# A two-layer transformer trunk on one NeuronCore: the second layer's feed-forward begun with five blocks ahead, its first products set among the sums of its operands, and its weight splits put on VectorE

## The chip, the core and the metric

The kernel runs on one NeuronCore of one Trainium2 chip. Five engines work side by side: TensorE (PE, matrix products), VectorE (DVE), ScalarE (ACT), GpSimd (POOL), and SyncE (SP), whose queue issues nearly all of the transfers here. Each engine takes its instructions in the order in which they stand in its program; one that waits holds up all behind it on that engine. The metric is the device time of one execution in microseconds (us). Three runs of the kernel before took 2861.15, 2862.23 and 2865.08 us; their median is 2862.23.

## The reference

The input is a sequence of 1024 tokens of 1024 features with a context of 256 tokens. Two layers, each a token mixer and a gated feed-forward, with residuals and a modulation by a condition; layer 0 mixes by latent attention and a chunked MLP, layer 1 by retention and window attention. All in float32. The change touches the end of layer 1:

```python
def _swiglu(x, w_in, w_out):
    a, b = jnp.split(x @ w_in, 2, axis=-1)
    return (jax.nn.silu(a) * b) @ w_out
# layer 1, where the context has no feed-forward any more
x = x + mx[2] * yx                                   # yx = (...) @ cd_out
x = x + mx[5] * _swiglu(_modulate(_rms(x, norm_ffn[layer]), mx[3], mx[4]), ffn_in[layer], ffn_out[layer])
return _rms(x, norm_final)
```

`w_in` is 1024 x 5632 (two halves of 2816), `w_out` 2816 x 1024.

## The kernel before

Features lie on partitions, tokens along the free dimension, in two chunks of 512 tokens (0 and 1). A float32 product is made of three matmuls: each operand is split into a high part (ScalarE, an Identity to float32r) and a low part (the difference, VectorE or GpSimd), and high x high, low x high and high x low are added up in one PSUM bank (`mm3`, L112 to L114). Every product of 128 x 128 by 128 x 512 is so three matmuls.

Layer 1's mixer ends in eight output blocks for each chunk (`MixerOut.block`, L801): 24 matmuls on a weight of 512 KB, an addition into x on VectorE (L808), a square on ScalarE (L198), and for chunk 1 five of the eight squares are added into one tile on GpSimd (L202). For each block a weight is loaded and split (`load_w`, L255): high part L103, low part L107 on VectorE or L109 on GpSimd.

The feed-forward of layer 1 uses a Strassen scheme of the Winograd kind: seven products of half size in place of eight. Its operands from x are seven combinations of the two chunks, here named B11 and B21 (from chunk 0 alone), and T2, T3, T1, T4, B22 (which need chunk 1 as well). Each has four tiles, each tile with a high and a low part: 12 matmuls for each operand and block. `Seven.second` (L1466) makes the last five one after the other: scalings (L1433), subtractions (L1471, L1477), high parts (ACT L1448) and low parts (DVE L1454, L1456).

The 2816 hidden features are 22 blocks j. The front of a block is its two products with B11 and B21 (`front_1`, `front_2`; ScalarE takes the first out in `front_s`, L1609, VectorE adds the second and ScalarE makes the gate in `front_3`, L1615 and L1616). Its later products are the five with T2, T3, T1, T4 and B22, in this order, three of them into the bank X, two into the bank Z. Between them X is read by ScalarE (L1730) after T2 and by VectorE (L1748) after T1, and Z by ScalarE (L1738) after T3 and by VectorE (L1751) after T4; L1758 and L1766 multiply by the gates. The weights of the five come from one load of 1 MB by class `Back`: `part2`, `comb` (four sums of rows, L1538), `part(4)`, `part(3)`, where part 3 serves T2 and B22, part 4 serves T3 and T1, part 2 serves T4. `split_1(j + 3)` splits the weights of a later front.

From `front_1(0)` to the end of the 22 blocks the order on every engine is that of the code (`tc.manual_schedule`); before and after it a scheduler of the framework sets it. In the manual part the order is: the fronts of blocks 0 to 2 (`LEAD = 3`) with the last sums of squares (L211) behind the first product; then weights of block 0 and the norm's factor; then the whole of `second`, with the first steps of the fronts put among it; then the loop over j (L1719), which makes the five later products of block j, prepares block j + 1, and makes the front of block j + 2 (for j > 0).

Then `fout` (L1790) multiplies by `w_out` in 42 steps of up to 24 matmuls. Each step has one load of up to 1 MB (`load_b`), one high part on ScalarE (L1676, 128 x 2048) and a low part of which half is made on GpSimd (L1677) and half on VectorE (L1678), two steps ahead (`split_b`). Steps 0 and 1 are loaded and split behind blocks 20 and 21.

```python
        if j >= NJ - 2:
            k = j - NJ + 2
            split_b(k, load_b(k))
```

x, which was spilled to DRAM, is loaded back at the start of `fout` (L1795), 2 MB for each chunk.

## Time and profile before

| | us |
|---|---|
| median of three runs | 2862.23 |
| the profiled execution, its own time | 2856.81 |
| its span from first to last instruction | 2855.0 |
| PE busy | 2673.5 (94%) |
| DVE busy | 1765.1 (62%) |
| ACT busy | 1036.4 (36%) |
| POOL busy | 852.2 (30%) |

A row of the timeline gives start, duration, engine, line, operation, output and inputs by name, shape and count, and in brackets the idle time of that engine just before and what ended it. SPq is SyncE's queue issuing a transfer. In a row of windows the numbers are the window, its length, and for each engine the busy time and the number of instructions, then the TensorE clock that was granted (1.00 is 2.4 GHz, 0.50 is 1.2 GHz), the share of the DMA engines and GB/s. Buffers are reused under their pool's names, so `w`, `wo`, `rx` stand for parts of x, `a` and `tx` for split operands and weights, and `ps` for any PSUM bank. Two records of one matmul may overlap; the distance from one start to the next is its cost.

### The profile page before, as it was taken

What the parts mean: (1) busy time and instruction counts of PE and PEld (TensorE: products, weight loads), DVE (VectorE), ACT (ScalarE), POOL (GpSimd) and SP (SyncE); (2) the same over time, 40 slices, a digit from 0 to 9 for tenths busy, and PEclk for the clock granted to TensorE, in tenths of its full rate; (3) what the DMA queues carried; (4) which work ended last, traced back from release to release, by engine and by line L of the source; (5) the groups of instructions that cost most, each with busy time, mean ns of one, the idle gap of its engine ahead of it and who ended that gap; (6) DMA issues with size and microseconds to landing.
All of it is one profiled execution on the core that took longest, in us unless ns stands there. A gap on an engine that the chain in (4) does not pass through costs nothing.

```text
span 2855.0 us, 35441 instructions
## 1 busy us (share of the span) xinstructions
PE 2673.5 (94%) x13524; PEld 2241.9 (79%) x13524; DVE 1765.1 (62%) x3137; ACT 1036.4 (36%) x1677; POOL 852.2 (30%) x513
## 2 busy tenths in 40 slices
...
GB/s 237 104 135 116 34 31 31 131 157 72 73 63 89 67 69 72 73 79 57 45 30 45 87 98 79 64 50 152 86 159 66 162 138 141 168 173 232 207 184 139
DMA packets 127643, 299.41 MB, mean 105 GB/s; under 512 B 12145, under 2 KB 28273, under 8 KB 126193
## 3 DMA queue, kind: packets, MB, share of 16 engines
...
## 4 chain that ended last, share of the span: by engine, by line
PE 61%; DVE 16%; DMA 6%; ACT 5%; issue 5%; POOL 5%; SPq 0%; DVEq 0%; ACTq 0%; POOLq 0%
PE ps L112 18%; PE ps L114 18%; PE ps L113 18%; DVE junk L149 3%; DMA adaw<-in_ada_dram 3%; POOL a L1677 1%; POOL tx L1677 1%; DVE t2k L233 1%; POOL wl L109 1%; PE ps L701 1%; DVE sm L1099 1%; DVE st L681 1%; DVE spt L107 1%; PE ps L191 1%; ACT P L684 1%
## 5 line engine op out<-in xcount | busy, mean ns | idle before, releaser
L112 PE MATMUL ps<-a,wh 128*128 128x512 f32 (+1 forms) x1784 | 656.7, 368 | 22.2 <-ACT wh L103 7.5
L113 PE MATMUL ps<-a,wl 128*128 128x512 f32 (+1 forms) x1784 | 649.7, 364 | 13.3 <-DVE wl L107 8.0
L114 PE MATMUL ps<-a,wh 128*128 128x512 f32 (+1 forms) x1784 | 647.2, 363 | 2.4 <-DVE a L239 1.8
L109 POOL TENSOR_TENSOR wl<-raw,wh 128x1024 fp32r<-128x1024 f32 x115 | 286.1, 2492 | 867.8 <-ACT wh L103 865.3
L112 PEld LDWEIGHTS ps<-a,wh 128*128 128x128 f32 x1784 | 342.5, 192 | 81.1 <-ACT wh L103 9.4
L113 PEld LDWEIGHTS ps<-a,wl 128*128 128x128 f32 x1784 | 342.5, 192 | 71.2 <-DVE wl L107 11.0
L114 PEld LDWEIGHTS ps<-a,wh 128*128 128x128 f32 x1784 | 341.9, 192 | 54.9 <-DVE a L239 3.1
L860 DVE SCALAR_TENSOR_TENSOR x<-ps,md,x 128x512 f32<-128x512 f32 (+1 forms) x528 | 312.3, 653 | 4.1 <-PE ps L114 4.1
L149 DVE CUSTOM_DVE_ANT_0 junk<-adaw,cond_x 128x512 bf16<-128x512 f32 x160 | 130.5, 816 | 171.8 <-DMA adaw<-in_ada_dram 170.0
L843 DVE TENSOR_TENSOR t2k<-t2k,ps 128x512 f32<-128x512 f32 (+1 forms) x66 | 39.4, 597 | 247.9 <-PE ps L114 247.9
L112 PE MATMUL ps<-hh,wh 128*128 128x512 f32 (+1 forms) x528 | 188.4, 357 | 3.5 <-ACT hh L103 2.5
L114 PE MATMUL ps<-hl,wh 128*128 128x512 f32 (+1 forms) x528 | 187.4, 356 | 1.0 <-DVE hl L107 1.0
L113 PE MATMUL ps<-hh,wl 128*128 128x512 f32 (+1 forms) x528 | 188.0, 356 | 0.0
L103 ACT ACTIVATE wh<-raw 128x1024 fp32r<-128x1024 f32 x127 | 134.1, 1057 | 115.2 <-PE ps L114 43.5
L842 ACT ACTIVATE t2k<-ps 128x512 f32<-128x512 f32 (+1 forms) x66 | 34.8, 527 | 383.8 <-PE ps L114 383.7
L114 PE MATMUL ps<-a,w 128*128 128x512 f32 x416 | 165.1, 397 | 5.9 <-DVE a L1456 5.9
L112 PE MATMUL ps<-a,w 128*128 128x512 f32 x416 | 164.7, 396 | 4.0 <-ACT a L1448 2.1
L113 PE MATMUL ps<-a,w 128*128 128x512 f32 x416 | 164.3, 395 | 0.0
L103 ACT ACTIVATE hh<-t2k 128x512 fp32r<-128x512 f32 (+1 forms) x66 | 36.8, 557 | 282.7 <-DVE t2k L843 282.7
L202 POOL TENSOR_TENSOR acc<-t2k,acc 128x512 f32<-128x512 f32 (+1 forms) x69 | 86.2, 1254 | 125.3 <-ACT t2k L198 123.7
L112 PEld LDWEIGHTS ps<-hh,wh 128*128 128x128 f32 x528 | 100.5, 190 | 18.9 <-ACT hh L103 2.9
L114 PEld LDWEIGHTS ps<-hl,wh 128*128 128x128 f32 x528 | 100.3, 190 | 15.5 <-DVE hl L107 1.5
...
## 6 DMA issues: line engine op xcount, KB each, us to landing
...
```

Source lines behind the costliest of these rows:

```text
L103: ac.activation(hi, src, AF.Identity)
L107: ve.tensor_tensor(lo, src, f32(hi), op=ALU.subtract)
L109: po.tensor_tensor(lo, src, f32(hi), op=ALU.subtract)
L112: te.matmul(ps, wh, xh, start=first, stop=False, skip_group_check=more)
L113: te.matmul(ps, wl, xh, start=False, stop=False, skip_group_check=more)
L114: te.matmul(ps, wh, xl, start=False, stop=last, skip_group_check=more)
L149: ve.tensor_tensor_reduce(jk[:, :512], w, cond[which][:, h * 512 : h * 512 + 512], op0=ALU.mult, op1=ALU.add, scale=1.0, scalar=0.0, accum ...
L202: po.tensor_tensor(self.acc[:, :n], sq[:, :n], self.acc[:, :n], op=ALU.add)
L842: ac.activation(s[:, :n], pa, AF.Silu)
L843: ve.tensor_tensor(s[:, :n], s[:, :n], pb, op=ALU.mult)
L860: ve.scalar_tensor_tensor(xm, ps[:, s], mod(l, which(c), GATE_F, m), xm, op0=ALU.mult, op1=ALU.add)
L1677: po.tensor_tensor(lo[:, 0, :n], raw[:, 0, :n], f32(hi[:, 0, :n]), op=ALU.subtract)
```

## The change

- `LEAD` is 5: five fronts are made ahead, not three. `pre_w` loads their weights beside output blocks 0 to 4 of chunk 1 (before: 2 to 4) into two buffers of their own (`fr`), not into the mixer's `raw`; block 0's load for its five later products is issued at output block 0, into other tiles.
- The low parts of the mixer's weights in chunk 1, of the front weights (`pre_w`, `split_1`) and of `split_b` are made on VectorE, not on GpSimd; so are the five additions of squares of chunk 1 (`mo.rm[1].eng = ve`). `split_b`'s low part is one VectorE instruction of 128 x 2048.
- The norm's factor of chunk 1 (`finish`) is ordered ahead of part 3 of block 0's weights.
- The later products of block 0 are made by a class `Block` and, with the first steps of the five fronts, placed by a table `plan` among the tiles of `second`. All but the last (B22) stand inside it.
- In the loop a front is made for j + 2 from block 5 on, so in j = 0, 1 and 2 none. The gate of a front is made in place, in ScalarE's copy of its first product.
- Loads and splits of `fout`'s steps 0 to 3 stand in blocks 20 and 21.

```diff
@@
-    LEAD = 3
+    LEAD = 5
     def pre_w(j):
-        wp, _, rb = wpools[j % 2]
-        raw = T(wp, [P, 1024], "raw", bufs=rb)
+        raw = T(pwB, [P, 1024], "fr", F32, 2)
         sy.dma_start(raw, A["w_fi"][L, j, 0])
-        w = t8([P, 2, 2, 512])
-        cut(w[:, 0], w[:, 1], raw.rearrange("p (a n) -> p a n", a=2), "pool")
+        w = t8([P, 2, 2, 512]) if j else act_tile(2, [P, 2, 2, 512])
+        cut(w[:, 0], w[:, 1], raw.rearrange("p (a n) -> p a n", a=2), "dve")
@@
+    mo.rm[1].eng = ve
     for m in range(KB):
         mo.block(m, 1, acts)
         spill(1, m)
-        if 2 <= m < 2 + LEAD:
-            pre_w(m - 2)
-        if m == 2 + LEAD:
+        if m < LEAD:
+            pre_w(m)
+        if m == 0:
             bk = Back(0, pre_raw())
@@
-        if j < NJ:
+        if LEAD <= j < NJ:
             w = T(pX, [P, 2, 2, 512], "w1", F32R, 2)
             W1[j] = w[:, 0], w[:, 1]
-            cut(w[:, 0], w[:, 1], raws[j][:, 0:2], "pool")
+            cut(w[:, 0], w[:, 1], raws[j][:, 0:2], "dve")
@@
-        po.tensor_tensor(lo[:, 0, :n], raw[:, 0, :n], f32(hi[:, 0, :n]), op=ALU.subtract)
-        ve.tensor_tensor(lo[:, 1, :n], raw[:, 1, :n], f32(hi[:, 1, :n]), op=ALU.subtract)
+        ve.tensor_tensor(lo[:, :, :n], raw[:, :, :n], f32(hi[:, :, :n]), op=ALU.subtract)
@@
+    mo.rm[1].finish(True)
     bk.part(3)
-    mo.rm[1].finish(True)
     bk.part(4)
     front_3(0)
@@
+    plan = {("T2", 0): [lambda: front_s(1)], ("T2", 1): [lambda: front_3(1), lambda: front_s(2)],
+            ("T2", 3): [lambda: front_3(2), lambda: front_s(3)], ("T3", 0): [lambda: front_3(3), bl.m6],
+            ("T3", 2): [lambda: front_s(4)], ("T1", 0): [lambda: front_3(4), bl.m7, bl.u1], ("T4", 0): [bl.m5],
+            ("T4", 2): [bl.z7], ("B22", 0): [bl.m4], ("B22", 1): [bl.c22]}
@@
+        if kb == 0:
+            braw = {k: load_b(k) for k in range(2)}
+        if kb == 1:
+            braw[2] = load_b(2)
...
+        if kb == 1:
+            split_b(1, braw[1])
+            braw[3] = load_b(3)
...
+        if kb == 1:
+            split_b(2, braw[2])
...
+        if kb == 0:
+            split_b(0, braw[0])
@@
-        if j >= NJ - 2:
-            k = j - NJ + 2
-            split_b(k, load_b(k))
...
+    split_b(3, braw[3])
@@
-            if k + 2 < len(steps):
+            if k > 1 and k + 2 < len(steps):
                 split_b(k + 2, load_b(k + 2))
```

In `plan`, `m6`, `m7`, `m5`, `m4` are the products with T2, T3, T1 and T4, `u1` and `z7` ScalarE's copies of X and Z, `c22` VectorE's sum on X.

Three places show how instructions move. The first is VectorE's order at the second half of chunk 1's output blocks: `w`, `wo` are x, `rx` too, `acc` the sum of squares, `wl` a weight's low part. Before:

```order
L1433 SCALAR_TENSOR_TENSOR rx_16946<-rx_16946,md_1792_9764,rstd_18129 128x512 x4
L1454 SCALAR_TENSOR_TENSOR a_3261_18139<-w_3021_16945,md_1970_10760,a_3261_18139 128x512 x4
L1454 SCALAR_TENSOR_TENSOR a_3262_18148<-rx_16946,md_1970_10760,a_3262_18148 128x512 x4
L808 SCALAR_TENSOR_TENSOR w_3023_16947<-ps_18161,md_1614_8769,w_3023_16947 128x512
L808 SCALAR_TENSOR_TENSOR w_3023_16947<-ps_18197,md_1614_8769,w_3023_16947 128x512
L808 SCALAR_TENSOR_TENSOR w_3023_16947<-ps_18238,md_1614_8769,w_3023_16947 128x512
```

And now:

```order
L1433 SCALAR_TENSOR_TENSOR rx_16946<-rx_16946,md_1792_9764,rstd_18129 128x512 x4
L1454 SCALAR_TENSOR_TENSOR a_3261_18139<-w_3021_16945,md_1970_10760,a_3261_18139 128x512 x4
L1454 SCALAR_TENSOR_TENSOR a_3262_18148<-rx_16946,md_1970_10760,a_3262_18148 128x512 x4
L809 SCALAR_TENSOR_TENSOR w_3023_16947<-ps_18169,md_1614_8769,w_3023_16947 128x512
L809 SCALAR_TENSOR_TENSOR w_3023_16947<-ps_18210,md_1614_8769,w_3023_16947 128x512
L107 TENSOR_TENSOR wl_18289<-raw_18286,wh_18288 128x1024
L203 TENSOR_TENSOR acc_18158<-t2k_18195,acc_18158 128x512
```

The low part of output block 4's weight (`wl_18289`) now stands on VectorE, behind the 16 instructions of the chunk 0 operands and two additions into x; the sums of squares stand there as well.

The second is ScalarE's order at the end of `second`. The outputs of L1448 are the high parts: before, `a_3340_18594`, `tx_18611`, `tx_18621` and `a_3347_18635` are those of T3, T1, T4 and B22; now `tx_18688`, `tx_18715` and `a_3357_18743` are those of T1, T4 and B22. Before:

```order
L1448 ACTIVATE a_3340_18594<-w_3023_16947 128x512 x4
L1448 ACTIVATE tx_18611<-w_3021_16945 128x512 x4
L1448 ACTIVATE tx_18621<-rx_16946 128x512 x4
L1448 ACTIVATE a_3347_18635<-wo_16948,md_1970_10760 128x512 x4
L1730 ACTIVATE acc_18662<-ps_18437 128x512
```

And now:

```order
L1615 ACTIVATE g_3349_18679<-g_3349_18679 128x512
L1717 ACTIVATE t2k_18705<-ps_18447 128x512
L1448 ACTIVATE tx_18688<-w_3021_16945 128x512 x4
L1448 ACTIVATE tx_18715<-rx_16946 128x512 x2
L1725 ACTIVATE t2k_18734<-ps_18692 128x512
L1448 ACTIVATE tx_18715<-rx_16946 128x512 x2
L1448 ACTIVATE a_3357_18743<-wo_16948,md_1970_10760 128x512 x4
```

The copy of X after T2 (L1730, now L1717) stood behind all high parts and stands now behind T3's; that of Z (now L1725) stands amid T4's.

The third is VectorE's order at the end of block 21. `a`, `tx` out of `raw`, `rx` are `fout`'s steps 0, 1, 2, 3 in this order. Before:

```order
L1678 TENSOR_TENSOR tx_21494<-rx_21489,tx_21493 128x1024
L1766 TENSOR_TENSOR t2k_21429<-t2k_21429,g_3699_21458 128x512
L1622 TENSOR_TENSOR t2k_21462<-t2k_21341,t2k_21355 128x512
L1623 TENSOR_TENSOR t2k_21341<-t2k_21429,t2k_21341 128x512
L1624 TENSOR_TENSOR t2k_21463<-t2k_21429,t2k_21462 128x512
L1625 TENSOR_TENSOR t2k_21464<-t2k_21443,t2k_21463 128x512
L1678 TENSOR_TENSOR a_3704_21473<-raw_21469,a_3704_21473 128x1024
```

And now:

```order
L1676 TENSOR_TENSOR a_3631_21309<-raw_21232,a_3631_21309 128x2048
L1748 TENSOR_TENSOR t2k_21272<-t2k_21272,g_3632_21328 128x512
L1676 TENSOR_TENSOR a_3637_21364<-raw_21236,a_3637_21364 128x2048
L1731 TENSOR_TENSOR t2k_21362<-ps_21139,t2k_21362 128x512
L1737 TENSOR_TENSOR t2k_21347<-ps_21349,t2k_21347 128x512
L1676 TENSOR_TENSOR tx_21398<-rx_21331,tx_21397 128x2048
L1740 TENSOR_TENSOR t2k_21347<-t2k_21347,ps_21180 128x512
```

Step 1's low part (`a_3704` before, `a_3637` now) stood behind block 21's last gate and the four hidden sums (L1622 to L1625), and stands now ahead of block 21's first VectorE sum.

## Rows read from the trace of the kernel before

**Rows 1.** The head of the profile's page.

```profile
span 2855.0 us, 35441 instructions
```

**Rows 2.** Windows: the output blocks of chunk 1; from the first front to the first T2 product of block 1; blocks 1 to 20; block 21 and the start of `fout`; steps of `fout`. Columns are window, length, busy time and count of PE, PE's weight loads, DVE, ACT, POOL, granted clock, DMA share, GB/s.

```profile
2098.50:2155.67 57.17, 49.15 (x196) 38.58 (x195) 27.46 (x27) 20.98 (x28) 27.63 (x14) 0.94 0.34 111
2155.67:2216.34 60.67, 42.22 (x139) 29.85 (x138) 49.80 (x67) 27.90 (x41) 8.04 (x4) 0.77 0.22 74
2216.34:2597.20 380.86, 380.86 (x1658) 311.52 (x1657) 221.98 (x280) 128.86 (x176) 105.29 (x58) 1.00 0.44 156
2597.20:2640.00 42.80, 33.39 (x134) 26.50 (x133) 21.28 (x16) 12.47 (x10) 17.16 (x8) 0.88 0.79 299
2640.00:2800.00 160.00, 160.00 (x706) 132.42 (x706) 72.41 (x54) 61.45 (x44) 106.99 (x43) 1.00 0.60 201
```

**Rows 3.** Timeline of PE in chunk 1's output blocks: the first two matmuls of blocks 4 and 6.

```profile
2123.83 0.51 PE L112 MATMUL ps<-a,wh 128*128 128x512 f32 x1 [1.40 <-ACT wh L103]
2126.32 0.50 PE L113 MATMUL ps<-a,wl 128*128 128x512 f32 x1 [1.98 <-POOL wl L109]
...
2140.83 0.51 PE L112 MATMUL ps<-a,wh 128*128 128x512 f32 x1 [1.96 <-ACT wh L103]
2143.26 0.50 PE L113 MATMUL ps<-a,wl 128*128 128x512 f32 x1 [1.92 <-POOL wl L109]
```

**Rows 4.** Timeline of DVE (the chunk 0 operands: eight scalings, then low parts) and of POOL (two front weights) in the same stretch.

```profile
2110.21 2.74 DVE L1433 SCALAR_TENSOR_TENSOR w<-w,md,rstd 128x512 f32<-128x512 f32 x4
2112.86 9.21 DVE L1433 SCALAR_TENSOR_TENSOR rx<-rx,md,rstd 128x512 f32<-128x512 f32 x4
2121.99 4.82 DVE L1454 SCALAR_TENSOR_TENSOR a<-w,md,a 128x512 fp32r<-128x512 f32 x4
...
2112.69 5.35 POOL L1415 TENSOR_TENSOR tx<-raw,tx 128x1024 fp32r<-128x1024 f32 x2 [5.29 <-ACT tx L1413]
```

**Rows 5.** Timeline of POOL, SP's queue and ACT on the weight of output block 6.

```profile
2132.18 2.43 POOL L1415 TENSOR_TENSOR tx<-raw,tx 128x1024 fp32r<-128x1024 f32 x1
...
2134.64 0.33 SPq L260 DMA_DIRECT2D raw<-in_w_cdo_dram  x1
...
2139.72 1.06 ACT L103 ACTIVATE wh<-raw 128x1024 fp32r<-128x1024 f32 x1 [4.83 <-DMA raw<-in_w_cdo_dram]
```

**Rows 6.** Timeline of ACT and DVE from the sums of squares to the end of `second`.

```profile
2161.23 0.63 ACT L1413 ACTIVATE w<-tx 128x512 fp32r<-128x512 f32 x1 [1.92 <-PE ps L211]
2168.01 0.69 ACT L223 ACTIVATE t2k<-ps,eps 128x512 f32<-128x512 f32 x1
...
2170.85 0.69 DVE L228 SCALAR_TENSOR_TENSOR g<-t2k,t2k 128x512 f32<-128x512 f32 x1
2173.19 0.74 DVE L1433 SCALAR_TENSOR_TENSOR w<-w,md,g 128x512 f32<-128x512 f32 x1
2185.85 1.47 DVE L1456 TENSOR_TENSOR a<-t2k,a 128x512 fp32r<-128x512 f32 x2
2201.04 2.74 DVE L1454 SCALAR_TENSOR_TENSOR a<-wo,md,a 128x512 fp32r<-128x512 f32 x4
```

**Rows 7.** Timeline of PE (first matmul of T2, of T1 and of T4 of block 0) and of ACT.

```profile
2176.70 0.50 PE L112 MATMUL ps<-a,w 128*128 128x512 f32 x1 [1.50 <-ACT a L1448]
2203.38 0.79 PE L112 MATMUL ps<-tx,w 128*128 128x512 f32 x1 [8.59 <-ACT acc L1730]
2208.67 0.42 PE L112 MATMUL ps<-tx,w 128*128 128x512 f32 x1
...
2202.75 0.57 ACT L1730 ACTIVATE acc<-ps 128x512 f32<-128x512 f32 x1
```

**Rows 8.** Timeline of DVE (the weights of block 1's later products: part 2, the second pair of row sums, part 3) and POOL.

```profile
2203.88 0.69 DVE L1415 TENSOR_TENSOR w<-raw,w 128x512 fp32r<-128x512 f32 x1
2208.30 4.57 DVE L1538 TENSOR_TENSOR raw<-raw 128x512 f32<-128x512 f32 x2
2214.04 1.23 DVE L1415 TENSOR_TENSOR w<-raw,w 128x1024 fp32r<-128x1024 f32 x1
...
2208.14 2.49 POOL L1415 TENSOR_TENSOR w<-rx,w 128x1024 fp32r<-128x1024 f32 x1 [63.70 <-ACT w L1413]
```

**Rows 9.** Timeline at the start of `fout`: PE at step 1, SP's queue on chunk 1 of x, ACT on step 4.

```profile
2617.14 0.49 PE L112 MATMUL ps<-a 128*128 128x512 f32 x1 [0.71 <-ACT a L1676]
2621.08 0.50 PE L113 MATMUL ps<-a 128*128 128x512 f32 x1 [3.45 <-POOL a L1677]
2626.84 0.79 PE L114 MATMUL ps<-a 128*128 128x512 f32 x1 [5.26 <-DVE a L1678]
...
2626.34 0.40 SPq L1795 DMA_DIRECT2D a<-xr  x1
...
2636.90 1.92 ACT L1676 ACTIVATE a<-raw 128x2048 fp32r<-128x2048 f32 x1 [18.03 <-DMA raw<-hd]
```

**Rows 10.** Timeline of PE late in `fout`: the sum of squares of chunk 0.

```profile
2807.36 1.12 PE L211 MATMUL ps<-acc,ones 128*128 128x512 f32 x2 [3.10 <-POOL acc L202]
```

**Rows 11.** Timeline of DVE and ACT at the end of an even block in the middle of the loop: Z's sum after T4, part 3 of the next block's weights, and ACT on X after B22.

```profile
2404.18 0.69 DVE L1751 TENSOR_TENSOR t2k<-ps,acc 128x512 f32<-128x512 f32 x1 [2.10 <-PE ps L114]
2404.79 2.23 DVE L1415 TENSOR_TENSOR w<-raw,w 128x1024 fp32r<-128x1024 f32 x1
...
2409.95 0.58 ACT L1765 ACTIVATE g<-ps 128x512 f32<-128x512 f32 x1
```

More of the change, by code (lines that the diff above doesn't have):

```diff
@@ L183, in __init__ @@
             self.summed = False
+            self.eng = po
         def add(self, src):
@@ L1693, in dit @@
     t2p[0] = pA
-    t2n.update(t2k=7, acc=3, g0=3)
-    t2a["rstd"] = "g0"
+    t2n.update(t2k=7, g0=6)
+    t2a.update(rstd="g0", acc="g0")
     load_fi(1)
@@ L1701, in dit, with __init__, m6, u1 @@
         bk.comb(i)
+    mo.rm[1].finish(True)
     bk.part(3)
-    mo.rm[1].finish(True)
     bk.part(4)
     front_3(0)
-    def at(name, k):
-        if name == "T2" and 0 < k < 3:
-            front_s(k)
-        if name == "T2" and k == 3:
-            front_3(1)
-        if name == "T3" and k == 0:
-            front_3(2)
+    class Block:
+        def __init__(self, j, w):
+            self.j, self.w = j, w
+            self.X, self.g0 = pre.pop(j)
+        def m6(self):
+            mm4(self.X, self.w.w3, 0, "T2", False, True)
+        def u1(self):
+            self.h0 = t2k()
+            ac.activation(self.h0, self.X, AF.Identity)
+        def m7(self):
+            self.Z = T(pp, [P, 512], "ps")
+            mm4(self.Z, self.w.w4, 0, "T3", True, True)
+        def z7(self):
+            self.h1 = t2k()
+            ac.activation(self.h1, self.Z, AF.Identity)
+        def m5(self):
+            mm4(self.X, self.w.w4, 1, "T1", False, True)
+        def c22(self):
+            ve.tensor_tensor(self.h1, self.X, self.h1, op=ALU.add)
+        def m4(self):
+            mm4(self.Z, self.w.w2, 0, "T4", False, True)
+        def c21(self):
+            ve.tensor_tensor(self.h0, self.Z, self.h0, op=ALU.add)
+        def gate0(self):
+            ve.tensor_tensor(self.h0, self.h0, self.g0, op=ALU.mult)
+        def m3(self):
+            mm4(self.X, self.w.w3, 1, "B22", False, True)
+        def gate1(self):
+            g1 = t2k("g0")
+            ac.activation(g1, self.X, AF.Silu)
+            ve.tensor_tensor(self.h1, self.h1, g1, op=ALU.mult)
+            hid[self.j] = self.h0, self.h1
+    bl = Block(0, bk)
+    plan = {("T2", 0): [lambda: front_s(1)], ("T2", 1): [lambda: front_3(1), lambda: front_s(2)],
+            ("T2", 3): [lambda: front_3(2), lambda: front_s(3)], ("T3", 0): [lambda: front_3(3), bl.m6],
+            ("T3", 2): [lambda: front_s(4)], ("T1", 0): [lambda: front_3(4), bl.m7, bl.u1], ("T4", 0): [bl.m5],
+            ("T4", 2): [bl.z7], ("B22", 0): [bl.m4], ("B22", 1): [bl.c22]}
+    def at(name, k):
+        for f_ in plan.get((name, k), ()):
+            f_()
     sv.second(mo.rm[1], t2k, at)
@@ L1719, in dit @@
     for j in range(NJ):
-        X, g0 = pre.pop(j)
-        f = j + 2 if j and j + 2 < NJ else None
+        f = j + 2 if LEAD <= j + 2 < NJ else None
         for o in outs_:
@@ L1745, in dit @@
             front_s(f)
-        mm4(X, bk.w4, 1, "T1", False, True)
-        h1 = t2k()
-        ve.tensor_tensor(h1, X, m7, op=ALU.add)
-        mm4(Z, bk.w2, 0, "T4", False, True)
-        h0 = t2k()
-        ve.tensor_tensor(h0, Z, u1, op=ALU.add)
+        if j:
+            bl.m5()
+            bl.c22()
+            bl.m4()
+        bl.c21()
+        if kb == 1:
+            split_b(2, braw[2])
         split_1(j + 3)
@@ L1762, in dit @@
             front_3(f)
-        mm4(X, bk.w3, 1, "B22", False, True)
-        g1 = T(pA, [P, 512], "g0", F32, 3)
-        ac.activation(g1, X, AF.Silu)
-        ve.tensor_tensor(h1, h1, g1, op=ALU.mult)
-        hid[j] = h0, h1
+        bl.m3()
+        bl.gate1()
         if j % 2:
```

31 lines of the change are left out of this document (15 added, 16 removed).

## The prediction, made before the changed kernel ran

> **What bounds the kernel now.** I read the page's busy times first: PE works 94% of a span of 2855.0 us [rows 1], so a change of order can save only where PE waits or runs at a lower clock. Second came windows over the stretches the diff touches, third the idle time ahead of PE's first matmuls and what ended it, then the chain of DVE, ACT, POOL and SyncE's queue behind it. The windows [rows 2] say where there is something to gain: blocks 1 to 20 and the steps of `fout` are full on PE at clock 1.00, and a matmul costs there 160.00/706 = 0.227 us (380.86/1658 = 0.230 in the blocks). In each other window I compare the length with the matmuls at 0.227: 57.17 against 196 x 0.227 = 44.5 us (12.7 lost, output blocks of chunk 1); 60.67 against 139 x 0.227 = 31.6 (29.1 lost, making the operands); 42.80 against 134 x 0.227 = 30.4 (12.4 lost, start of `fout`). These 54 us and one wait of 3.10 us [rows 10] are the most the change can reach.
>
> **Output blocks of chunk 1.** The lost 12.7 us are four waits, 1.40 + 1.98 + 1.96 + 1.92 = 7.3 us [rows 3], a clock of 0.94 over 57.17 us, 3.4 us, and 2 us of small gaps. Both pairs have one cause. While POOL makes a front's low parts (5.35 us for two), DVE crawls: four scalings of chunk 0's operands take 2.74 us before it, the next four 9.21 beside it [rows 4]. And the last such split holds the shared buffer `raw`, so that the weight of block 6 is asked for at 2134.64, as POOL ends (2132.18 + 2.43), and is split at 2139.72 [rows 5]. The change puts front weights into buffers of their own and off POOL, so both go.
>
> It adds a wait: block 4's low part now stands on DVE behind 16 instructions and two additions. Alone the 16 take 0.67 each (2.74/4), an addition of that form 0.74 (2173.19 [rows 6]), the low part 1.23 (128 x 1024 [rows 8]): 2110.21 + 16 x 0.67 + 2 x 0.74 + 1.23 = 2123.6. PE ran dry at 2123.83 - 1.40 = 2122.43 [rows 3], so 1.2 us of wait are left; I take 1.3. Behind that low part DVE holds only the next blocks' additions and low parts. The two further loads of 512 KB are issued at blocks 0 and 1, in a stretch with a DMA share of 0.34 [rows 2]; I take them at nothing. All five front splits (5 x 1.23 us) and five additions of squares (0.69 each, as L1751 [rows 11]), 9.6 us, come on a DVE that is busy 27.46 of 57.17 us, and lose most of the POOL neighbour; I take them at nothing too, but if none hides the price is 9.6. Gain 10.7 - 1.3 = **9.4 us**: the fronts begin at 2146.3 in place of 2155.67.
>
> On this the Trainium skill, "Perfetto Trace Analysis", section "Optimizing Scalar/DVE Operations", says that GPSIMD and DVE share an SBUF read port, so that moving work between those two might not help, and that a saturated DVE may be relieved by others. The 9.21 against 2.74 us agree that the two hold each other up. By the rule the move from POOL would gain nothing where DVE is the fuller one.
>
> **Making the operands.** The sums of squares are released by ACT 5.6 us after the first front (2161.23 - 2155.67 [rows 6]), now at 2151.9. Before, the first scaling with the new factor began 12.0 us later (2173.19), behind part 3 of block 0's weights. Now the factor comes first: from the logarithm (2168.01) to the end of L228 (2170.85 + 0.69) are 3.5 us, plus two splits of 1.23 and a gate's addition of 0.69 ahead of the scaling, 6.7 us: 2158.6. From there DVE's chain to the end of B22's low parts was 2173.19 to 2201.04 + 2.74 = 2203.78, 30.6 us. Two more gates' additions and X's sum, 0.69 each, make 32.6: it ends at 2191.2. The first T2 product started 3.5 us after the first scaling (2176.70 [rows 7]), but needs all tiles to go on: T2's last low parts end 14.1 us after it (2185.85 + 1.47 - 2173.19), so 2158.6 + 14.1 + 0.7 = 2173.4. PE is busy until then: before, three fronts took from 2155.67 to 2176.70 - 1.50 = 2175.20, 19.5 us; two more are 48 x 0.227 = 10.9 us, until 2176.7. So PE runs from the fronts into T2 without a gap. The later products then go at the pace of DVE's subtractions. The wait of 8.59 us ahead of T1 was ACT's copy of X (L1730, at 2202.75 [rows 7]), queued behind every high part; it now stands behind T3's.
>
> After 2191.2 DVE makes the weights of block 1. Before, that took from 2203.78 to the end of part 3 (2214.04 + 1.23 = 2215.27 [rows 8]): 11.5 us. POOL's split of a later front beside it (2.49) stretched two row sums to 4.57 where two splits of that size take 1.4: 3.2 us go. The sum on X, 0.7, goes too since it has been made; the row sums for `w_out` on POOL stay beside part 3, whose 1.23 then becomes 2.23 [rows 11]: 1.0 comes. So 11.5 - 3.2 - 0.7 + 1.0 = 8.6, and block 1's T2 is at 2199.8 instead of 2216.34: 16.5 us sooner, 9.4 of them the first stage's. Of the work behind it, 48 matmuls have been done ahead: 10.9 us less. Against that: PE, done with block 0 soon after 2191.2, waits some 8 us for these weights, and the matmuls behind such a wait ran at half clock (12 from 2203.38 to 2208.67, 5.29 us in place of 2.7 [rows 7]): 2.6 us. And block 2, which has no front beside it either, needs in the 2.7 us of its 12 T4 matmuls on DVE a sum (0.69), a split and part 3 (1.23 to 2.23 each), 3.2 to 5.2 us: 0.5 to 2.4 us of wait, I take 1.5, the middle. Gain 16.5 - 9.4 + 10.9 - 2.6 - 1.5 = **13.9 us**.
>
> **The blocks between.** PE is full there [rows 2], so moving `split_1` from POOL to DVE gains nothing. It can cost: DVE must make a split of 1.23 to 2.23 us more ahead of part 3, which the next T2 needs. In the middle of the loop part 3 ended at 2404.79 + 2.23 = 2407.02, and ACT reads X after B22, the last product ahead of T2, at 2409.95 [rows 11]: 2.9 us of room. The split fits at either end of its price, so I take nothing.
>
> **The start of `fout`.** 12.4 us are lost, mainly at step 1: 0.71 + 3.45 + 5.26 = 9.4 us, ended by ACT, POOL and DVE in turn [rows 9]; the low part stands behind block 21's gate and sums. With steps 0 to 3 loaded and split inside blocks 20 and 21 the waits go, with a clock of 0.88: gain **12.4 us**. What is late next is step 4: its load stands behind x's 4 MB; its data came 10.6 us after x's second load was issued (2626.34 to 2636.90), then 1.92 for the high part and 2 x 1.23 for a low part of this size. Steps 0 to 3 give PE about 96 x 0.227 = 21.8 us; the data is ready about 1.5 us before PE gets there. Late in `fout`, with a DVE that adds the squares, the wait of 3.10 us on POOL's sum falls to about 0.3: **2.8 us**.
>
> **Sum.** 9.4 + 13.9 + 12.4 + 2.8 = 38.5. The profiled execution took 2856.81 us in all, which makes 2818.3. The median of the three runs is 2862.23, 5.4 above it; the same difference gives **2823.7, rounded 2824 us**.
>
> **Rivals.** *DVE becomes the bound ahead of the fronts.* For it: the 9.6 us of new work, a wait for a low part behind 16 instructions, and 49.80 us busy of 60.67 in the next stage. Against it: it loses the neighbour that made it three times slower. The first stage then gains nothing: 2824 + 9.4 = 2833 us. By the sentence on the shared read port it would go this way if POOL's part had been cheap; the rows say that it was not.
>
> *`fout`'s steps 4 and 5 wait for data.* x's 4 MB stand on the same queue, and 1.5 us of room is little; the DMA share is 0.79 there. Against it: steps 0 to 3 are now asked for 20 us and more earlier. From 5 to 12 of the 12.4 us come back: 2829 to 2836.
>
> *More goes than I count.* The waits left in (1.3, 1.5, 2.6 and the 8 us for block 1's weights) may vanish as DVE is quicker alone: about 2811.
>
> *Slower.* The split on DVE makes part 3 late in each of 17 blocks (those that split for fronts 5 to 21). It decides from 38.5/17 = 2.3 us beyond the room of 2.9, that is where a split costs over 5.2 us; at 3 beyond it is 17 x 3 = 51 lost, 2824 + 51 = 2875. For it: DVE doubles some of its times beside POOL (2.23 against 1.23). Against it: DVE is busy only 221.98 of 380.86 us there, and loses half its rivalry with POOL with this very move.
>
> *No change.* Within 0.2% (5.7 us, about what a measurement of this kernel can tell from no change): the gains of the first two stages would have to be eaten by a new wait at block 1 and the third by x's loads. That the order stays as it was is ruled out by the rows in the three places of the change.
>
> **How the numbers follow.** My forecast has 52 in 100, with a range of its own of 2814 to 2833 (unknown terms: 1.3, 1.5 and 2.6 either way, the clock, and up to 9.6 of DVE's new work). DVE as the bound has 16, `fout` late 14, more than counted 10, slower 5, no change 3. The range takes in DVE's bound and `fout`'s, and one of these beside part of the other: 2810 to 2842. Faster 0.92, same 0.03, slower 0.05.
>
> **What would show it.** Right: the first front near 2146 and no wait of over 1.5 us in chunk 1's output blocks; T2 behind the fronts without a gap; no wait of PE on the copy of X; T2 of block 1 near 2200; blocks 2 to 20 full on PE; PE without a gap at steps 0 to 4; the sum of squares (L211) late in `fout` without its 3 us. Wrong: PE waiting for `wl` of DVE in the output blocks; PE idle ahead of T2 of block 1 by far over 8 us; waits on DVE's `w` ahead of each T2; ACT waiting on `hd` at step 4.

## The result, and the profile after

The changed kernel took 2820.78 us (median of four runs, 2819.12 to 2822.97) against 2861.69 for four runs of the kernel before: ratio 0.9863, interval 0.9837 to 0.989, that is 31 to 47 us less. Forecast were 2824 us, 2810 to 2842, and faster at 0.92.

Runs of one kernel lie up to 14 us apart (2851.49 to 2865.77 for the kernel before, over all runs), so single stages are compared inside the traces, from one mark that both have: the start of the last matmul on `qcat` of layer 1's mixer, at 2042.26 us before and 2043.76 now. The table gives the time from it to the first front, to ScalarE's gate of block 3 (its reading of X after B22, L1747), to the late sum of squares (L211, now L212) and to the end.

| from the mark, us | first front | gate of block 3 | sum of squares | end |
|---|---|---|---|---|
| before | 113.4 | 232.2 | 765.1 | 812.8 |
| changed | 102.5 | 211.8 | 729.1 | 777.4 |
| gained in the stage | 10.9 | 9.6 | 15.5 | -0.6 |
| forecast for the stage | 9.4 | 13.9 | 15.2 in all | |

The windows of the changed kernel, with the columns of [rows 2]: chunk 1's output blocks, from the first front to block 1's first product, the 6.9 us behind that, block 2, blocks 4 to 19, and the last block with `fout`'s first steps.

```profile
2098.50:2146.29 47.79, 45.74 (x198) 36.84 (x197) 30.94 (x40) 19.95 (x27) 1.48 (x1) 1.00 0.33 113
2146.29:2199.40 53.11, 45.38 (x188) 34.47 (x186) 45.39 (x68) 29.25 (x45) 1.38 (x2) 0.98 0.24 84
2199.40:2206.30 6.90, 5.36 (x12) 3.90 (x13) 5.64 (x3) 0.43 (x1) 4.93 (x3) 0.50 0.45 152
...
2220.00:2233.11 13.11, 9.56 (x42) 7.18 (x40) 7.38 (x12) 4.10 (x6) 0.00 (x0) 1.00 0.97 350
...
2255.52:2560.00 304.48, 304.48 (x1326) 249.10 (x1325) 194.16 (x237) 101.50 (x142) 55.50 (x32) 1.00 0.44 159
...
2574.00:2616.80 42.80, 42.80 (x189) 35.27 (x188) 24.54 (x21) 15.58 (x12) 7.98 (x4) 1.00 0.90 340
```

Where the kernel before had clocks of 0.94, 0.77 and 0.88 [rows 2] there is now 1.00, 0.98 and 1.00. What is left stands between 2199 and 2233: 6.9 us at half clock with 12 matmuls, and a block in which PE has work for 9.56 of 13.11 us while the DMA engines are full (0.97). The timeline of the changed kernel shows the waits: PE, then what stood behind them on DVE, POOL, ACT and SP's queue, and some rows that are used further below.

```profile
2124.83 0.50 PE L113 MATMUL ps<-a,wl 128*128 128x512 f32 x1 [1.24 <-DVE wl L107]
...
2146.29 0.39 PE L112 MATMUL ps<-a,a 128*128 128x512 f32 x1
...
2199.40 0.79 PE L112 MATMUL ps<-a,w 128*128 128x512 f32 x1 [6.35 <-ACT w L1413]
2201.73 0.80 PE L113 MATMUL ps<-a,w 128*128 128x512 f32 x1 [1.54 <-DVE w L1415]
...
2228.97 0.50 PE L112 MATMUL ps<-tx,w 128*128 128x512 f32 x1 [2.47 <-ACT t2k L1725]
...
2233.11 0.51 PE L112 MATMUL ps<-a,w 128*128 128x512 f32 x1 [1.08 <-DVE t2k L1731]
...
2772.88 0.70 PE L212 MATMUL ps<-g,ones 128*128 128x512 f32 x1 [0.71 <-POOL g L203]
...
2158.28 0.74 DVE L1433 SCALAR_TENSOR_TENSOR w<-w,md,g 128x512 f32<-128x512 f32 x1
...
2181.28 2.50 DVE L1456 TENSOR_TENSOR tx<-w,tx 128x512 fp32r<-128x512 f32 x4 [1.70 <-ACT tx L1448]
...
2189.66 2.73 DVE L1454 SCALAR_TENSOR_TENSOR a<-wo,md,a 128x512 fp32r<-128x512 f32 x4
...
2199.38 2.30 DVE L1415 TENSOR_TENSOR w<-raw,w 128x1024 fp32r<-128x1024 f32 x1 [0.66 <-ACT w L1413]
...
2197.94 6.55 POOL L1537 TENSOR_TENSOR wo<-wo 128x512 f32<-128x512 f32 x4 [94.64 <-DMA wo<-in_w_fo_dram]
...
2179.61 0.63 ACT L1615 ACTIVATE g<-g 128x512 f32<-128x512 f32 x1 [1.36 <-DVE g L1614]
...
2228.32 0.60 ACT L1725 ACTIVATE t2k<-ps 128x512 f32<-128x512 f32 x1 [6.18 <-DMA hd<-t2k]
...
2218.39 0.58 SPq L1644 DMA_DIRECT2D sd<-wo  x1
2219.01 3.25 SPq L1629 DMA_DIRECT2D hd<-t2k  x3
...
2609.52 1.92 ACT L1675 ACTIVATE a<-raw 128x2048 fp32r<-128x2048 f32 x1 [14.82 <-DMA raw<-hd]
...
2253.50 0.69 DVE L1614 TENSOR_TENSOR ps<-g,ps 128x512 f32<-128x512 f32 x1
```

PE's 2.47 us in block 2 look like ScalarE's doing (L1725, the copy of Z). ScalarE itself had waited 6.18 us, and not for PE: its output tile `t2k` was still being stored (`hd<-t2k`, issued at 2219.01 behind the 1 MB of `sd<-wo`). A releaser is to be followed until something is named that was itself busy.

The last row corrects the part on the change: a front's gate is made in place in ScalarE's copy for the five early fronts alone; from front 5 on it lies in the PSUM bank of the second product (`ps<-g,ps`), since there the copy is taken ahead of that product.

### The profile page after: what moved, and what is told of

It is laid out like the page before. It is cut to its first block, busy times and chain, and to the rows that moved or that the text cites. A ratio compares the mean times of both kernels' runs of the same rounds, so it can differ in the third digit from the quotient of the medians.

```text
span 2821.2 us, 35301 instructions
## 1 busy us (share of the span) xinstructions
PE 2663.8 (94%) x13524; PEld 2237.7 (79%) x13524; DVE 1802.2 (64%) x3170; ACT 1033.1 (37%) x1677; POOL 668.3 (24%) x438
## 4 chain that ended last, share of the span: by engine, by line
PE 68%; DVE 16%; DMA 6%; ACT 5%; issue 3%; POOL 2%; SPq 0%; DVEq 0%; ACTq 0%; POOLq 0%
PE ps L112 21%; PE ps L113 21%; PE ps L114 21%; DVE junk L149 3%; DMA adaw<-in_ada_dram 2%; PE ps L702 1%; DVE sm L1100 1%; DVE t2k L234 1%; DVE st L682 1%; DVE spt L107 1%; ACT P L685 1%; PE ps L192 1%; POOL wl L109 1%; DMA t2k<-oc 1%; ACT wh L103 1%
## 5 line engine op out<-in xcount | busy, mean ns | idle before, releaser
L109 POOL TENSOR_TENSOR wl<-raw,wh 128x1024 fp32r<-128x1024 f32 x109 | 269.0, 2471 | 863.2 <-ACT wh L103 856.7
L149 DVE CUSTOM_DVE_ANT_0 junk<-adaw,cond_x 128x512 bf16<-128x512 f32 x160 | 137.9, 862 | 171.6 <-DMA adaw<-in_ada_dram 169.7
L1537 POOL TENSOR_TENSOR wo<-wo 128x512 f32<-128x512 f32 x44 | 76.9, 1749 | 403.4 <-DMA wo<-in_w_fo_dram 400.8
L112 PE MATMUL ps<-a,w 128*128 128x512 f32 x400 | 158.0, 395 | 7.6 <-ACT w L1413 6.3
L113 PE MATMUL ps<-a,w 128*128 128x512 f32 x400 | 157.8, 395 | 1.5 <-DVE w L1415 1.5
L114 PE MATMUL ps<-a,w 128*128 128x512 f32 x400 | 157.6, 394 | 0.0
L112 PEld LDWEIGHTS ps<-hh,wh 128*128 128x128 f32 x528 | 100.6, 190 | 18.5 <-ACT hh L103 2.6
```

The costliest lines, as they stand in the source:

```text
L109: po.tensor_tensor(lo, src, f32(hi), op=ALU.subtract)
L112: te.matmul(ps, wh, xh, start=first, stop=False, skip_group_check=more)
L113: te.matmul(ps, wl, xh, start=False, stop=False, skip_group_check=more)
L114: te.matmul(ps, wh, xl, start=False, stop=last, skip_group_check=more)
L149: ve.tensor_tensor_reduce(jk[:, :512], w, cond[which][:, h * 512 : h * 512 + 512], op0=ALU.mult, op1=ALU.add, scale=1.0, scalar=0.0, accum ...
L1537: e.tensor_tensor(self.rows(o, o + 1), self.rows(a, a + 1), self.rows(b, b + 1), op=op)
```

## The experiments

Times from the mark are those of each run's trace, ratios those of the runs with the kernel before on the same chip.

| run | ratio, interval | first front | gate of block 3 | sum of squares | end |
|---|---|---|---|---|---|
| e1_tail_only | 0.993, 0.9915 to 0.9945 | 114.2 | 233.1 | 750.4 | 798.7 |
| e2_fronts_pool | 0.9865, 0.9848 to 0.9881 | 102.9 | 211.7 | 729.1 | 777.3 |
| e3_lead3 | 0.9876, 0.9862 to 0.9891 | 100.0 | 213.6 | 731.3 | 779.5 |
| e4_dummy | 0.9839, 0.9824 to 0.9854 | 101.5 | 206.6 | 725.6 | 773.8 |
| e5_allpool | 0.9878, 0.986 to 0.9895 | 101.5 | 210.2 | 728.2 | 776.5 |
| e6_hid_first | 0.9882, 0.9867 to 0.9898 | 104.2 | 208.9 | 733.2 | 781.5 |
| e7_split1_pool | 0.9897, 0.9881 to 0.9913 | 104.2 | 216.3 | 733.7 | 782.0 |
| e8_combo | 0.9891, 0.9873 to 0.9909 | 101.9 | 207.6 | 730.0 | 778.3 |
| e9_before_fr | 0.996, 0.9945 to 0.9975 | 100.8 | 221.2 | 752.9 | 802.2 |
| e10_after_again | 0.9871, 0.9853 to 0.9888 | 104.7 | 212.0 | 729.3 | 777.6 |
| e11_hid0_x1 | 0.986, 0.9844 to 0.9875 | 103.9 | 208.8 | 726.2 | 774.4 |
| e12_best | 0.9848, 0.9833 to 0.9862 | 100.7 | 202.7 | 720.0 | 768.3 |

The changed kernel repeated without any edit (e10) reaches the first front 2.1 us later than in its first trace, but the gate of block 2 and all that is read behind it within 0.3. The lateness is gone by then, mostly since two waits are shorter in e10: that for the low part in block 1 by 1.07 us, that in block 2 by 0.41. So 2 us at the first front decide nothing, and a stage counted from the first front can come out 2 us different with nothing changed. From the mark to block 3 and behind, the two traces agree to 0.2 us; I take 1 us there as a difference, though two traces are few.

> The changed kernel unaltered, for comparison on one chip with the next two: 2817 to 2824 us, PE's waits in blocks 1 to 3 as in its first trace (about 6.3, 1.5, 2.5 and 1.1 us).

**The end of the blocks alone.** In the kernel before, `fout`'s steps 0 to 3 are loaded and split as in the changed one.

```diff
+        if kb == 0:
+            braw = {k: load_b(k) for k in range(2)}
...
-            split_b(k, load_b(k))
...
+            if k > 1 and k + 2 < len(steps):
```

> The kernel before with one part of the change alone: fout's steps 0 to 3 are loaded and split inside blocks 20 and 21, each low part one VectorE instruction of 128 x 2048. My theory (the gains of the stages are separate and add up): the start of fout loses its 12.4 us of waits and the late sum of squares some 2 us, so 13 to 15 us less than before, the rest of the trace as before. Rival A (the tail gains only because the stage ahead of it ends earlier and x's loads meet a freer queue): 5 us or less. Rival B (step 4 then waits for data behind x's 4 MB): 12.4 - 5 to 12, that is 0 to 7 us less, with ScalarE waiting on hd at step 4.

The end comes 14.1 us sooner (812.8 to 798.7), the sum of squares 14.7; up to block 3 the trace is that of the kernel before, 0.8 us later. From the gate of block 3 to the end it takes 565.6 us, as the changed kernel does (580.6 before). Where 134 matmuls were made in 42.80 us [rows 2], a window of that length has 191 at full clock, and the 3.10 us of [rows 10] are 0.70, though GpSimd still adds the squares there, now without `split_b`'s half beside them.

```profile
2615.10:2657.90 42.80, 42.80 (x191) 35.42 (x190) 24.42 (x20) 15.93 (x10) 0.00 (x0) 1.00 0.88 326
```

```profile
2796.20 1.13 PE L211 MATMUL ps<-acc,ones 128*128 128x512 f32 x2 [0.70 <-POOL acc L202]
```

**The engine of the low parts in the output blocks.** First the front weights alone, then those and the mixer's go back to GpSimd in the changed kernel.

```diff
-        cut(w[:, 0], w[:, 1], raw.rearrange("p (a n) -> p a n", a=2), "dve")
+        cut(w[:, 0], w[:, 1], raw.rearrange("p (a n) -> p a n", a=2), "pool")
```

```diff
     mo.load(1)
+    mo.leng = "pool"
```

> The changed kernel with the low parts of the five early front weights back on GpSimd; their own buffers, and the mixer's low parts on VectorE, stay. My theory (GpSimd's splits slow VectorE's scalings of chunk 0's operands to about a third of their speed): the 16 instructions ahead of block 4's low part take 5 to 8 us longer, PE's wait there grows from 1.24 us to 5 to 9 us, and the kernel is 4 to 8 us slower than the changed one. Rival (what the change removed was the wait on the shared buffer, not the contention): within 1.5 us of the changed kernel, wait there still near 1.2 us.

> The changed kernel with all low parts of chunk 1's output blocks back on GpSimd, those of the mixer's weights and those of the five front weights; the fronts' own buffers, their earlier places and the sums on VectorE stay. Theory after the run with the front weights alone on GpSimd (the front weights cost nothing there since they now run ahead of VectorE's 16 instructions; what hurts is any GpSimd split beside those 16, about 2.9 in place of 0.75 us for each VectorE instruction that it meets): the mixer's splits of blocks 4 and 5 fall beside the 16, the operands of chunk 0 come some 6 us later, PE waits 2 us each at blocks 4 to 6 on GpSimd's low parts, 3 to 7 us slower than the changed kernel. Rival (buffers and places made the whole first gain, the engine is indifferent): within 1.5 us.

Both rivals held: the fronts begin 0.4 us later and 1.1 us sooner, the end differs by 0.1 and 0.9. In the first run the front splits, at their new places, were done ahead of the 16 instructions, so it said nothing on the contention. In the second, GpSimd's splits did hit them; the windows and the timeline of e5_allpool (DVE, POOL):

```profile
2104.40:2149.34 44.94, 44.58 (x194) 36.24 (x195) 29.21 (x31) 19.56 (x27) 21.35 (x9) 1.00 0.33 116
```

```profile
2118.91 4.23 DVE L1434 SCALAR_TENSOR_TENSOR rx<-rx,md,rstd 128x512 f32<-128x512 f32 x3
...
2119.58 3.02 POOL L109 TENSOR_TENSOR wl<-raw,wh 128x1024 fp32r<-128x1024 f32 x1 [4.66 <-ACT wh L103]
```

Three scalings take 4.23 us where four took 2.74 alone [rows 4], and PE, busy 44.58 of 44.94 us, does not notice.

**The buffers alone.** In the kernel before, the three front weights get buffers of their own; their places in the program and the engines stay.

```diff
-        raw = T(wp, [P, 1024], "raw", bufs=rb)
+        raw = T(pwB, [P, 1024], "fr", F32, 2)
```

> The kernel before with one edit: the three early front weights are loaded into two buffers of their own, not into the mixer's shared buffer; they stay at output blocks 2 to 4 and their low parts on GpSimd. Theory after the runs with everything on GpSimd (buffers and places, not the engine, made the first gain): block 6's two waits (1.96 + 1.92 us) go, and with them part of the clock; block 4's two (1.40 + 1.98) go too if its load had also stood behind the shared buffer, and stay if the front weights' place beside the 16 VectorE instructions made them. So 4 to 6 us less than before if only the buffer of block 6 counts, 8 to 10 if the buffer is the whole cause. Rival (the engine after all): under 2 us.

The fronts begin 12.6 us sooner, more than in the changed kernel. The windows and the timeline of e9_before_fr (DVE, SP's queue and ACT on the weight of output block 4):

```profile
2101.28:2145.62 44.34, 44.34 (x194) 36.33 (x195) 24.07 (x26) 18.09 (x25) 20.37 (x11) 1.00 0.26 84
```

```profile
2114.44 7.04 DVE L1433 SCALAR_TENSOR_TENSOR rx<-rx,md,rstd 128x512 f32<-128x512 f32 x4
...
2108.90 0.33 SPq L260 DMA_DIRECT2D raw<-in_w_cdo_dram  x1
...
2112.98 1.06 ACT L103 ACTIVATE wh<-raw 128x1024 fp32r<-128x1024 f32 x1 [2.75 <-DMA raw<-in_w_cdo_dram]
```

PE is full with the clock at 1.00 while VectorE crawls nearly as before (7.04 us for four, 9.21 in [rows 4]). Outside the manual part the order is the scheduler's, and with buffers of their own the front splits ran earlier, ahead of the scalings; what these now meet on GpSimd are splits of the mixer's weights. So the buffers alone are enough for the whole first gain. That the slow scalings cost the kernel before nothing does not follow. There, the weight of output block 4 was asked for at 2115.25 and had landed 3.5 us later, but ScalarE split it at 2122.73 only, behind high parts of chunk 0's operands for which it had waited for VectorE's scalings. The timeline of the kernel before (SP's queue, ACT):

```profile
2115.25 3.15 SPq L260 DMA_DIRECT2D raw<-in_w_cdo_dram  x2
...
2121.44 1.39 ACT L1448 ACTIVATE a<-rx,md 128x512 fp32r<-128x512 f32 x2 [2.09 <-DVE rx L1433]
2122.73 1.04 ACT L103 ACTIVATE wh<-raw 128x1024 fp32r<-128x1024 f32 x1
```

In e9 the same weight is split at 2112.98, as it lands, ahead of those high parts. What faster scalings alone would have been worth, with the shared buffer kept, no run shows. Of e9's 12.6 us 1.6 are given back by block 3, and the end is 10.6 us sooner.

**Three fronts ahead, not five.**

```diff
-    LEAD = 5
+    LEAD = 3
```

(and in `plan` the steps of fronts 3 and 4 go)

> The changed kernel with three fronts ahead in place of five (blocks 1 and 2 make those of blocks 3 and 4). Theory (making the operands is bound by VectorE's chain, and PE's work ahead of it fills idle time): block 1's first product stays within 2 us of 2199.4 and the 48 matmuls, 10.9 us, come back in blocks 1 and 2, less the 3.5 us of waits in block 2 that the fronts then cover and 1.4 us for two gates' additions: 4 to 8 us slower than the changed kernel. Rival (fronts ahead only move PE's work, the idle time moves with it): within 2 us.

2.1 us slower in the trace, at the rival's edge and below the 4 to 8; by the medians on one chip it is 3.9 slower than e2. Block 1's first product did not stay: it came at 2194.97, its low part at 2198.26. Counted from the first front, which is itself 2.6 us sooner, that is 2.7 and 1.7 us sooner than in the changed kernel. The timeline of e3_lead3 (PE, DVE):

```profile
2194.97 0.80 PE L112 MATMUL ps<-a,w 128*128 128x512 f32 x1 [6.26 <-ACT w L1413]
2198.26 0.80 PE L113 MATMUL ps<-a,w 128*128 128x512 f32 x1 [2.50 <-DVE w L1415]
...
2176.93 2.50 DVE L1456 TENSOR_TENSOR tx<-w,tx 128x512 fp32r<-128x512 f32 x4 [0.31 <-ACT tx L1448]
```

So VectorE's chain is not independent of the fronts. Up to B22's low parts it is 2.6 us shorter: 1.2 us are the two gates' additions that are gone, and VectorE waits 0.31 us for T1's high parts in place of 1.70. ScalarE's copy of X stands ahead of these high parts, and with five fronts it comes behind the fifth front's gate (L1615 at 2179.61, for which ScalarE waits 1.36 us) and behind T2's products, which PE ends about then too (the last begins at 2179.20). With three fronts both are earlier; which of them alone would do, no run shows.

**PE kept busy through the wait of 6.35 us.** 24 products more, into a bank that nobody reads.

```diff
+        if j == 0:
+            dum = T(pp, [P, 512], "ps")
+            for r in range(2):
+                mm4(dum, bk.w3, r, "T2", True, True)
```

> The changed kernel with 24 more matmuls behind block 0's last product, on operands that are there, into a bank that nobody reads: they fill 5.4 of the 6.35 us in which PE waits for block 1's weights. Theory (the matmuls after that wait run at half clock because PE stood idle, which costs 3.0 us): the granted clock behind the wait is 1.00 or close to it, and the kernel is 2 to 3 us faster than the changed one although PE does more work. Rival (the half clock has another cause, or the wait for the low part at 2201.7 absorbs it): clock 0.50 as in the changed kernel, time within 1 us of it or 1 us slower.

3.6 us sooner at the end, 5.2 at block 3. The clock behind the wait rose to 0.75, not to 1.00: eight matmuls still came at half rate; the windows and the timeline of e4_dummy (PE):

```profile
2191.88:2198.80 6.92, 5.97 (x18) 4.55 (x19) 4.76 (x3) 1.49 (x3) 5.68 (x4) 0.75 0.42 152
```

```profile
2191.88 0.50 PE L112 MATMUL ps<-a,w 128*128 128x512 f32 x1 [0.88 <-ACT w L1413]
...
2217.34 0.50 PE L112 MATMUL ps<-tx,w 128*128 128x512 f32 x1 [0.34 <-ACT t2k L1725]
...
2604.39 0.50 PE L113 MATMUL ps<-a 128*128 128x512 f32 x1 [1.13 <-DVE a L1676]
```

Not all of it is the clock: the wait in block 2 fell from 2.47 to 0.34 as well. And a new one of 1.13 stands in `fout`.

**The order of two stores.**

```diff
         for o in outs_:
             hid_out(*o)
+        if outs_:
+            wo_store(j // 2 - 1)
...
-            wo_store(j // 2)
```

> The changed kernel with one order changed on SyncE's queue: a pair's store of w_out sums (1 MB) is issued behind the seven stores of hidden sums, not ahead of them. Theory (ScalarE's copy of Z in block 2 waited 6.18 us for a buffer of which the store had not landed, behind 2 MB of other transfers at a DMA share of 0.97, and that made PE's two waits of 2.47 and 1.08 us): ScalarE's wait falls by the time of 1 MB, about 3 us, and PE's two waits to under 1 us together: 2 to 3.5 us faster. Rival (the copy is late by VectorE or by the half clock, the buffer only came last by chance): the waits stay, time within 1 us.

The theory held where it was made: no wait from 2200 to 2560, and block 3 is reached 2.9 us sooner. But around `fout`'s first steps more is given back (7.0 us, 208.9 to 733.2 against 211.8 to 729.1), and the end comes 4.1 us later. The windows and the timeline of e6_hid_first (PE):

```profile
2200.00:2560.00 360.00, 360.00 (x1559) 293.80 (x1558) 221.76 (x283) 120.33 (x165) 55.22 (x38) 1.00 0.44 153
```

```profile
2578.13 0.50 PE L112 MATMUL ps<-a 128*128 128x512 f32 x1 [1.39 <-ACT a L1675]
...
2610.45 1.20 PE L112 MATMUL ps<-a 128*128 128x512 f32 x4 [1.88 <-ACT a L1675]
```

**The later front weights on GpSimd again** (`split_1`: `"dve"` to `"pool"`).

> The changed kernel with the low parts of the later front weights (blocks 2 to 18) back on GpSimd. Theory (PE is full in the blocks, the split is hidden on either engine): blocks 3 to 20 have the same length, time within 1 us. Rival A (beside GpSimd VectorE's part 3 comes late): waits ahead of T2, 5 us slower or more. Rival B (VectorE in the changed kernel is the hidden bound): faster by over 2 us.

From the gate of block 5 to that of block 19 it takes 270.4 us, as the changed kernel does to 0.01: in the full blocks the engine costs nothing. But it is 4.5 us slower at the end. Its fronts began 1.7 us later, but at the gate of block 1 it stands where the changed kernel does (174.5 us from the mark in both); from there to the gate of block 2 it takes 22.1 us in place of 17.9. Block 2 has no front. GpSimd's split falls there beside two row sums of VectorE, which take 3.58 us (1.41 in the changed kernel); the sum on X behind them is late, and PE waits 3.24 us for it in place of 1.08. The matmuls behind that wait ran at half clock. None of the three accounts had that. The windows and the timeline of e7_split1_pool (PE, DVE, POOL):

```profile
2231.70:2237.20 5.50, 5.50 (x13) 4.34 (x14) 3.54 (x3) 0.57 (x1) 5.26 (x4) 0.50 0.48 150
```

```profile
2225.39 0.50 PE L112 MATMUL ps<-tx,w 128*128 128x512 f32 x1 [2.08 <-ACT t2k L1725]
...
2231.70 0.79 PE L112 MATMUL ps<-a,w 128*128 128x512 f32 x1 [3.24 <-DVE t2k L1731]
...
2227.46 3.58 DVE L1537 TENSOR_TENSOR rx<-rx 128x512 f32<-128x512 f32 x2
...
2227.32 2.45 POOL L1415 TENSOR_TENSOR w<-raw,w 128x1024 fp32r<-128x1024 f32 x1 [23.72 <-ACT w L1413]
```

**Combinations.** e8 has the dummies, the stores in the new order for all pairs, and

```diff
+        if j == 0:
+            wo_load(0)
```

behind block 1's part 3, in place of the loop's head.

> The changed kernel with three edits together: the 24 idle matmuls behind block 0, the hidden sums stored ahead of the sums of w_out, and block 0's load of w_out (on which GpSimd's row sums run beside VectorE's last split of block 1) behind that split. Theory: 3 us from the clock, up to 1 from GpSimd (2.30 to 1.23 us), and up to 3 from the buffer, of which the dummies gave about 2 already: 5 to 7 us faster than the changed kernel, block 1's low part of the first weights (2201.73) some 1 us earlier, no PE wait over 1 us after it. Rival (they cover the same idle time): as with the dummies alone, 2 to 4 us faster.

Block 3 is reached 4.2 us sooner, less than with the dummies alone (5.2), and 5.1 go again at `fout`: a miss. The load's new place moved GpSimd's row sums away from VectorE's last split of block 1's weights, but beside VectorE's row sums in block 1, which take 3.46 us in place of 1.4, and PE waits there. The timeline of e8_combo (PE, DVE, POOL):

```profile
2214.25 0.50 PE L112 MATMUL ps<-a,w 128*128 128x512 f32 x1 [1.92 <-DVE t2k L1731]
...
2210.13 3.46 DVE L1537 TENSOR_TENSOR raw<-raw 128x512 f32<-128x512 f32 x2
...
2207.83 6.90 POOL L1537 TENSOR_TENSOR wo<-wo 128x512 f32<-128x512 f32 x4 [105.97 <-DVE raw L1537]
```

e11 and e12 change the order of the stores for the first pair alone, and load chunk 1 of x later.

```diff
+        if j == 2:
+            wo_store(0)
...
+            if k == 6:
+                sy.dma_start(x[1], xr[1])
```

> The changed kernel with two moves on SyncE's queue: for the first pair of blocks alone the hidden sums are stored ahead of the sums of w_out, and chunk 1 of x is loaded at fout's step 6, not ahead of step 4's load. Theory: the first takes away the waits of 2.47 and 1.08 us (3.5 us, as with the same move for all pairs), the second keeps the gain, since step 4 no longer stands behind x's second 2 MB: no PE wait on ScalarE or VectorE (L1675, L1676) in fout's first steps, 2.5 to 4 us faster than the changed kernel. Rival (steps 4 and 5 are late for another reason, the last pair's own stores): a wait of 1 us or more stays there and eats 1.5 us or more.

> As the last one, with the 24 idle matmuls behind block 0's last product as well. Theory: the dummies give 3 us by the clock and the buffer's wait is mostly covered by the other move, so block 3 is reached 5.5 to 6.5 us sooner than in the changed kernel and nothing is given back in fout: 5 to 6.5 us faster, near 2815 us. Rival (the two cover the same wait, and fout takes some back): 3 to 4 us, as with the dummies alone.

e11 is 3.0 us faster in the trace and keeps it: at block 3, at the sum of squares and at the end. e12 is 9.1 us ahead of the changed kernel's first trace, 1.9 of them at the first front already; whether such a lead lasts is open, since e10's lag of 2.1 us did not. By the medians on one chip it is 7.2 us faster (2816.78 against e10's 2823.94), more than the 5 to 6.5 of the theory. Their ranges do not touch (2814.14 to 2817.64, 2821.02 to 2825.48). The window of e11_hid0_x1 behind block 1's first product, and VectorE's low part there:

```profile
2198.05:2204.95 6.90, 5.36 (x12) 3.89 (x13) 5.64 (x3) 0.43 (x1) 4.93 (x3) 0.50 0.45 152
```

```profile
2198.03 2.29 DVE L1415 TENSOR_TENSOR w<-raw,w 128x1024 fp32r<-128x1024 f32 x1 [0.66 <-ACT w L1413]
```

And of e12_best:

```profile
2199.93:2206.30 6.37, 5.37 (x22) 4.23 (x23) 5.73 (x4) 1.55 (x3) 5.75 (x4) 1.00 0.50 165
```

```profile
2199.90 1.46 DVE L1415 TENSOR_TENSOR w<-raw,w 128x1024 fp32r<-128x1024 f32 x1 [0.66 <-ACT w L1413]
```

The programs differ by the dummies alone: a clock of 0.50 against 1.00, and from the first front to block 3 105.0 against 102.0 us. All of these 3.0 us lie between the gates of blocks 0 and 1 (18.5 and 15.5 us). Not all are the clock's: the low part took 1.46 in place of 2.29 us, beside GpSimd's row sums in both, and so came 0.8 us sooner; why, no run shows. The other 2.1 are 11 matmuls in 4.74 us in place of 2.62.

## Why the prediction was right, and where it was not

**Output blocks: the size right, the cause half wrong.** The wait that it left in was 1.24 us (1.3 forecast); the 0.67 us for each of the 16 instructions held too (10.62 us from 2111.62 to 2122.24), though 2.74/4 is 0.685. The stage gained 10.9 us (9.4); that the first front came at 2146.29 (2146.3) is luck, since the trace was 1.5 us late at the mark already. The step "Both pairs have one cause" fell in its first half: that GpSimd beside VectorE by itself costs PE something there. e9 and e5 keep the slow scalings, and PE does not wait for them. Its second half, the weight asked for only when the shared buffer came free [rows 5], is all of it for block 6's pair. At block 4's pair both stood in a row, the late load and then ScalarE behind the slow scalings; the load alone, made earlier, takes that wait away (e9). The move to VectorE added the 1.24 us, and up to 2.4 in e10 and e7. The sentence of the Trainium skill ("Perfetto Trace Analysis", section "Optimizing Scalar/DVE Operations"), that moving work between GPSIMD and DVE might not help, agrees with e2 and e5 (0.1 and 0.9 us); e7's 4.2 us in block 2 are a place where it did help. The rival of a VectorE that becomes the bound did not come true here.

**Making the operands: the mechanism right, 4.3 us too much.** VectorE's first scaling came at 2158.28 (2158.6). PE went from the fronts into T2 without a gap, at 2176.68 (2176.7), and the wait for ACT's copy of X is gone (one of 1.19 us for its copy of Z, at 2186.30, has come). Then three terms of the sum were too small. The low part that block 1's first product needs ended at 2199.38 + 2.30 = 2201.68, not 2199.8: 1.9 us. Of these 1.2 were in VectorE's chain (2189.66 + 2.73 = 2192.39 against 2191.2), where no term stood for the 1.70 us that it waited for T1's high parts, and 0.7 in the weights, where it waited 0.66 us for ScalarE's high part. The half clock cost 2.8 us (2.6): 13 matmuls in 5.71 us from 2201.73 on, which take 2.95 at 0.227. The transition of block 2 cost 2.47 + 1.08 = 3.55 (1.5), and the step named the wrong engine: I had VectorE in it, while it was a store that had not left its buffer; no term spoke of `hd`. 1.9 + 0.2 + 2.0 = 4.1 of the 4.3 that lie between 13.9 and 9.6; but e10 gains 11.5 in the same stage, so tenths prove nothing. That five fronts ahead are worth two more of 10.9 us was also too much: e3 has them at 2.1 at the end, for with them VectorE's chain is 2.6 us longer.

**The blocks between: right.** e7 shows it for blocks 6 to 19. At block 2, which has no front, the split's engine was worth 4.2 us; no term spoke of that.

**`fout`: right in size, and the margin as small as it was called.** 15.5 - 0.6 = 14.9 against 12.4 + 2.8 = 15.2, and e1 gets the same alone (580.6 to 565.6 us from the gate of block 3): the stages add up. One reason was wrong: late in `fout` it is still GpSimd that adds the squares (L203), not VectorE; free of the low parts, it keeps PE 0.71 us in place of 3.10. ScalarE waited 14.82 us for step 4's data and PE just did not: that low part was done 21.5 us after the gate of block 21, and PE wanted it, by e4, after 22.6, so there were 1.1 us of room (1.5 forecast). In e4 and e6 the late data cost 1.13 us and more, and with x's second 2 MB behind it (e11, e12) nothing. That rival was real, and 1 us away.

**The sum**: 10.9 + 9.6 + 14.9 = 35.4 from the mark against 38.5, and 1.5 us were lost ahead of it, where both kernels do the same. The medians differ by 40.9: runs scatter by more than the error of the sum. That the median came within 2.9 us of 2823.7 while the traces gained 3.1 less than forecast is luck.
